# A hybrid encoder block on one core: the order of the steps in an attention slot, and of the first loads and squares

## The chip, the cores and the metric

The kernel runs on one core of one Trainium2 chip, in one launch. The metric is the device time of that launch in microseconds (us), lower is better. TensorE (PE in the profile) multiplies matrices from SBUF into PSUM; its weight loads have a row of their own (PEld). ScalarE (ACT) and VectorE (DVE) read and write both memories. SyncE (SP) issues all loads and stores. Each engine works through its own queue in order, and semaphores tie the queues together.

## The reference

One encoder block on x (1024 tokens by 1024 features, float32), one layer:

```
h = rms_norm(x);  proj = h @ w_in          # 13 projections in one product
y_gla = gated linear attention, forward and backward, 4 heads, chunked
y_swa = softmax attention in a window of +-128, 8 heads on 2 key/value heads
x = x + (sigmoid(gate_a) * y_gla + sigmoid(gate_b) * y_swa) @ w_out
x = x + swiglu(rms_norm(x))                # feed-forward of width 2816
```

The softmax attention works on blocks of 128 queries, each against its own block of keys and the two beside it, with normed and rotated q and k and a learned sink logit per head:

```
scores = q . k / sqrt(128), masked to the window
m = max(scores.max, sink);  p = exp(scores - m)
o = (p / (p.sum + exp(sink - m))) @ v
```

## The kernel before, in words

**Arithmetic.** Every float32 matrix product is done as three matmuls. An operand a is split into a high part (ScalarE copies it into a rounded type, `wh`, `xh`, `qh`, `ph`) and a low part (VectorE subtracts the high part from the original, `wl`, `xl`, `ql`, `pl`), and `mm3` (lines 74 to 77) adds high x high, high x low and low x high in PSUM. `wunit` (lines 62 to 69) loads one weight tile of 128 x 512 and splits it so.

**Engines' orders.** Nearly all is written inside `tc.manual_schedule(engines={PE})`: TensorE's order is the order of the program text. The other engines' instructions are ordered by a scheduler at build time, from readiness and their place in the text. Tiles of a pool with one tag share `bufs` buffers; a new tile waits until an old one's last reader is done. PSUM holds two tags of four banks each: `mm` for the dense products and `ch` for the small ones.

**First stage (lines 263 to 306).** x is held transposed, as 8 feature tiles k by 2 halves s of 512 tokens, 256 KB each. For each k and s, `x_tile` loads the half tile, ScalarE makes `xh` (line 266, with the norm's gain as a scale), VectorE makes `xl` (line 267), ScalarE squares x (line 271) and VectorE adds the square to `acc` (line 273). TensorE then does 6 matmuls for the half tile: the first two dense projections (q and k of head 0), three matmuls each. The weight tiles of these two are loaded ahead of k = 0 and of k = 4 (line 279). After the loop come the low-rank gate product (`lr_mm`, 24 matmuls on line 72 into `ch`, in two halves), and between the halves the norm's statistics: a matmul of ones with `acc` (line 120, `norm_stats`).

**Dense work as filler.** All further projections are generators in the list `dense`. `fill(n)` takes the next n dense matmuls from it. `slot(stages, n)` (lines 230 to 238) runs the given stages one after the other and after each of them puts its share of n dense matmuls, so that TensorE has work while the other engines prepare the next stage. The gated linear attention (lines 310 to 502) and the softmax attention are both run in this way. Weight tiles of the dense work are loaded and split two tiles ahead (`next_unit`, lines 158 to 161).

**Softmax attention (lines 505 to 683).** The units are 16 pairs (g, n): a group g of four heads and a block n of 128 queries. One pair passes through six slots:

- slot n: `k_prep` (keys and values of the block, only while g = 0): load, value split, norm and rotation
- slot n + 1: `a_prep`: load of the four heads' q, sum of squares (line 531), rotation into `a.qn` (lines 587 to 592); `k_turn` (g = 0): transposes of the key block (line 573) and their split
- slot n + 2: `a_turn`: four transposes of q (line 598) and their split into `a.qh`, `a.ql`
- slot n + 3: `a_scores`, four stages, one per head: three matmuls into a bank (line 614), then VectorE adds the band mask, writes p and takes the row maximum (line 615). After the fourth head: the maximum with the sink (lines 622 to 624), four exponentials on ScalarE (line 630), the sum and its reciprocal on VectorE (lines 632 and 634), and four scalings of p on ScalarE (line 636)
- slot n + 4: `a_probs`, three stages, one per key block: four transposes of p (line 647), split into `ph` (ScalarE, line 650) and `pl` (VectorE, line 651)
- slot n + 5: `a_out`: nine matmuls of p with the values, a copy by ScalarE (line 661) and four stores

A slot thus holds stages of up to six different pairs. Their order within the slot is the tuple `order` (line 677), by which each slot's list is sorted (line 680). A slot has 46 dense matmuls, 60 in the first two and 28 in the last four. With g = 0 there are 12 stages in a slot, with g = 1 ten. p (line 605) and the row maxima (line 606) have two buffers each.

The rest, the two output projections, the merge, and the feed-forward block (done with seven products in place of eight per pair of blocks), follows from line 686 on and is not touched.

Of the kernel before, what the change touches and what calls it, by code (L numbers as in the profile page):

```python
# [8 lines left out]
F32 = mybir.dt.float32  # L9
FR = mybir.dt.float32r  # L10
U32 = mybir.dt.uint32
AF = mybir.ActivationFunctionType
ALU = mybir.AluOpType

P = 128
T = 1024
KT = 8
HT = 512
# [11 lines left out]
def body(tc, i, out):  # L30
    nc = tc.nc
    with ExitStack() as root:
# [8 lines left out]
        def nm(s):  # L41
            uid[0] += 1
            return f"{s}_{uid[0]}"

        def mmtile(shape=(P, 512), dt=F32):
            return psm.tile(list(shape), dt, tag="mm", name=nm("mm"))

        def chtile(shape, dt=F32):
            return psc.tile(list(shape), dt, tag="ch", name=nm("ch"))
# [7 lines left out]
        def load_const(pool, name, src, shape, dt=F32):  # L57
            t = pool.tile(list(shape), dt, tag=name, name=name)
            nc.sync.dma_start(out=t, in_=src)
            return t  # L60

        def wunit(src, n=512):
            raw = wp.tile([P, n], F32, tag="wr", name=nm("wr"), bufs=4)
            nc.sync.dma_start(out=raw, in_=src)
            h = wp.tile([P, n], FR, tag="wh", name=nm("wh"), bufs=5)
            nc.scalar.activation(h, raw, AF.Copy)  # L66
            l = wp.tile([P, n], FR, tag="wl", name=nm("wl"), bufs=5)
            nc.vector.tensor_tensor(l, raw, h.bitcast(F32), op=ALU.subtract)  # L68
            return h, l

        def mm(o, a, b, start, stop):
            nc.tensor.matmul(o, a, b, start=start, stop=stop)  # L72

        def mm3(o, ah, al, bh, bl, start, stop):
            mm(o, ah, bh, start, False)
            mm(o, ah, bl, False, False)
            mm(o, al, bh, False, stop)
# [3 lines left out]
        g1 = load_const(cst, "g1", i["g1"], (P, KT))  # L81
# [26 lines left out]
        xh = [[xp.tile([P, HT], FR, tag=f"xh{k}{s}", name=f"xh{k}{s}") for s in range(2)] for k in range(KT)]  # L108
        xl = [[xp.tile([P, HT], FR, tag=f"xl{k}{s}", name=f"xl{k}{s}") for s in range(2)] for k in range(KT)]
# [5 lines left out]
        ip = ini.enter_context(tc.tile_pool(name="ip", bufs=1))  # L115
# [131 lines left out]
        def lr_mm(b, u):  # L247
            h, l = wunit(i["w_lr"][u], 384)
            for kk in range(4):
                k = u * 4 + kk  # L250
                c = slice(kk * 96, (kk + 1) * 96)
                for s in range(2):
                    mm3(b[s][:96], h[:, c], l[:, c], xh[k][s], xl[k][s], k == 0, k == KT - 1)

        def lr_out(b):
# [4 lines left out]
            nc.scalar.activation(lrS[0:96], lrf, AF.Copy)  # L260
            nc.vector.tensor_tensor(lrS[32:64], lrf[32:64], lrS[32:64].bitcast(F32), op=ALU.subtract)

        def x_tile(k, s):
            xr = ip.tile([P, HT], F32, tag="xr", name=nm("xr"), bufs=8)
            nc.sync.dma_start(out=xr, in_=i["xT"][k, s])
            nc.scalar.activation(xh[k][s], xr, AF.Copy, scale=g1[:, k:k + 1])  # L266
            nc.vector.scalar_tensor_tensor(xl[k][s], xr, g1[:, k:k + 1], xh[k][s].bitcast(F32),  # L267
                                           op0=ALU.mult, op1=ALU.subtract)
            a = acc[:, s * HT:(s + 1) * HT]
            sq = a if k == 0 else ip.tile([P, HT], F32, tag="sq", name=nm("sq"), bufs=3)  # L270
            nc.scalar.activation(sq, xr, AF.Square)
            if k:
                nc.vector.tensor_tensor(a, a, sq, op=ALU.add)

        with tc.manual_schedule(engines={mybir.EngineType.PE}):
            bq = [[mmtile(), mmtile()] for _ in range(2)]
            for k in range(KT):
                if k % 4 == 0:
                    us = [wunit(i["w_f"][m, k // 4]) for m in range(2)]
                c = slice((k % 4) * P, (k % 4 + 1) * P)  # L280
                for s in range(2):
                    x_tile(k, s)
                    for m in range(2):
                        mm3(bq[m][s], us[m][0][:, c], us[m][1][:, c], xh[k][s], xl[k][s], k == 0, k == KT - 1)
            ident = load_const(cst, "ident", i["c_ident"], (P, P))
            tri = load_const(gc, "tri", i["c_tri"], (P, P), U32)
            g2 = load_const(cst, "g2", i["g2"], (P, KT))
            og = load_const(cst, "og", i["og"], (P, 2))
            bl = [chtile((P, 512)), chtile((P, 512))]
            lr_mm(bl, 0)  # L290
            norm_stats(acc, ip)
            vt = chtile((P, KT, 2))
            for t in range(KT):
                mm(vt[:, t], acc[:, t * P:(t + 1) * P], ones[:, 0:2], True, True)
            lr_mm(bl, 1)
            proj_f_out("q0", bq[0])
            proj_f_out("k0", bq[1])
            rsqrt(rstdt, vt[:, :, 0], 1.0 / T, EPS, epst, ip, (P, KT), "rt")
            upr = ip.tile([98, 2, 512], F32, tag="upr", name="upr")
            nc.sync.dma_start(out=upr, in_=i["up"])  # L300
            nc.scalar.activation(upS, upr, AF.Copy)
            nc.vector.tensor_tensor(upS[64:98], upr[64:98], upS[64:98].bitcast(F32), op=ALU.subtract)
            nc.scalar.activation(upS[96:97], upr[96:97], AF.Copy)
            nc.vector.memset(lrS[96:98].bitcast(F32), 1.0)
            lr_out(bl)
# [201 lines left out]
        sw = swas.enter_context(tc.tile_pool(name="swt", bufs=2))  # L507
# [86 lines left out]
        def a_turn(g, n):  # L594
            a = att[g, n]
            qt = chtile((P, 4, P))
            for h in range(4):
                nc.tensor.transpose(qt[:, h], a.qn[:, h], ident)
            a.qh = sw.tile([P, 4, P], FR, tag="qh", name=nm("sqh"))
            a.ql = sw.tile([P, 4, P], FR, tag="ql", name=nm("sql"))  # L600
            nc.scalar.activation(a.qh, qt, AF.Copy)
            nc.vector.tensor_tensor(a.ql, qt, a.qh.bitcast(F32), op=ALU.subtract)
            a.b0, a.b1 = max(n - 1, 0), min(n + 1, KT - 1)
            a.w = (a.b1 - a.b0 + 1) * P
            a.p = sw.tile([P, 4, 384], F32, tag="p", name=nm("p"))
            a.mx = sw.tile([P, 4], F32, tag="mx", name=nm("mx"))

        def a_scores(g, n, h):
            a = att[g, n]
            w, p, mx = a.w, a.p, a.mx  # L610
            ks = slice(a.b0 * P, (a.b1 + 1) * P)
            mo = (a.b0 - (n - 1)) * P
            s = chtile((P, 384))
            mm3(s[:, :w], a.qh[:, h], a.ql[:, h], kTh[:, g, ks], kTl[:, g, ks], True, True)
            nc.vector.tensor_tensor_reduce(out=p[:, h, :w], in0=s[:, :w], in1=band[:, mo:mo + w],
                                           op0=ALU.add, op1=ALU.max, scale=1.0, scalar=-1e30,
                                           accum_out=mx[:, h:h + 1])
            if h < 3:
                return
            sk = sink[:, 4 * g:4 * g + 4]  # L620
            nm_ = sw.tile([P, 4], F32, tag="nm", name=nm("nm"))
            nc.vector.tensor_tensor(mx, mx, a.rs, op=ALU.mult)
            nc.vector.tensor_tensor(mx, mx, sk, op=ALU.max)
            nc.vector.tensor_scalar(nm_, mx, -1.0, None, op0=ALU.mult)  # L624
            es = sw.tile([P, 4], F32, tag="es", name=nm("es"))
            nc.vector.tensor_tensor(es, sk, mx, op=ALU.subtract)
            nc.scalar.activation(es, es, AF.Exp)
            dn = sw.tile([P, 4], F32, tag="dn", name=nm("dn"))
            for h in range(4):
                nc.scalar.activation(p[:, h, :w], p[:, h, :w], AF.Exp, bias=nm_[:, h:h + 1],  # L630
                                     scale=a.rs[:, h:h + 1], accum_out=dn[:, h:h + 1])
            nc.vector.tensor_tensor(dn, dn, es, op=ALU.add)
            rd = sw.tile([P, 4], F32, tag="rd", name=nm("rd"))
            nc.vector.reciprocal(rd, dn)
            for h in range(4):
                nc.scalar.activation(p[:, h, :w], p[:, h, :w], AF.Copy, scale=rd[:, h:h + 1])  # L636
# [30 lines left out]
        for n in range(2 * KT):  # L667
# [6 lines left out]
            if n < KT:  # L674
                todo[n + 1].append((k_turn, n))
                todo[n].append((k_prep, n))
        order = (a_out, a_probs, a_scores, a_turn, k_turn, k_prep, a_prep)
        with tc.manual_schedule(engines={mybir.EngineType.PE}):
            for t, v in enumerate(todo):
                v.sort(key=lambda e: order.index(e[0]))  # L680
# [514 lines left out]
```

## Time and profile before

| what | value |
|---|---|
| median of 3 runs | 1697.69 us (1697.48 to 1699.71) |
| the profiled execution | 1697.71 us |
| its span, first to last instruction | 1695.6 us |
| TensorE matmuls busy | 1675.2 us, 7880 instructions |
| weight loads busy | 1388.9 us |
| VectorE busy | 1179.8 us |
| ScalarE busy | 867.8 us |

The first stage runs up to about 50 us, the gated linear attention to about 440 us, the softmax attention to about 750 us, the output projections to about 1070 us, the feed-forward block to the end.

In the rows of a timeline the first number is the start in us from the span's start, the second the duration of the row in us, then the engine, the source line, the operation, what is written and what is read, the shapes and the number of merged instructions; in square brackets stands how long the engine had been idle and what let it go. In the groups by line, the numbers behind the bar are busy us, mean ns of one instruction, and idle us of the engine just before them with what ended it. A matmul's shown duration is longer than the distance to the next one's start, since matmuls overlap in the array; lost time on TensorE is read best from starts.

### The profile page before, as it was taken

The page shows a single profiled execution, that of the slowest core. Times are in us where ns is not written, and L with a number is a line of the kernel's source. Part 1 is how long each engine was busy: PE and PEld are TensorE (multiplying, and loading weights), DVE is VectorE, ACT ScalarE, POOL GpSimd, SP SyncE. Part 2 cuts the span into 40 slices and gives each one's busy share as a digit, 9 for nine tenths or more (in the row PEclk, how much of TensorE's full clock was granted, in tenths as well). Part 3 has the DMA queues.
Part 4 walks back from the last instruction along what each step waited for, and adds up shares of the span by engine and source line. Part 5 has one row for each costly group of instructions (what it writes and reads, how often), then busy time and mean ns, then how long its engine had stood idle before and what let it go on. Part 6 is the DMA issues. An engine that isn't in the chain of part 4 may idle for free.

```text
span 1695.6 us, 23682 instructions
## 1 busy us (share of the span) xinstructions
PE 1675.2 (99%) x7880; PEld 1388.9 (82%) x7880; DVE 1179.8 (70%) x2454; ACT 867.8 (51%) x1939; POOL 0.2 (0%) x4
## 2 busy tenths in 40 slices
PE   8999999999999999999999999999999999999999
PEld 6788888888788878878888888888888888788887
DVE  7767777764577656537574468978778887779655
ACT  6554767775557565545453456633333333354443
POOL 0000000000000000000000000000000000000000
PEclk9999999999999999999999999999999999999999
DMA  6533444443543232237765645344223543496433
GB/s 196 156 112 111 121 130 135 132 143 119 177 128 108 82 106 81 82 108 249 237 200 168 192 137 180 116 128 149 88 94 131 172 157 129 138 342 200 142 106 118
DMA packets 153738, 245.85 MB, mean 145 GB/s; under 512 B 17582, under 2 KB 43054, under 8 KB 153616
## 3 DMA queue, kind: packets, MB, share of 16 engines
q1 hardware_dynamic: 153616, 244.34, 45.4%
q8 instruction: 62, 1.02, 0.3%
q14 instruction: 60, 0.49, 0.1%
HBM read 177.17 MB, written 67.11 MB: 144 GB/s over the span
## 4 chain that ended last, share of the span: by engine, by line
PE 92%; DVE 3%; ACT 3%; DMA 1%; issue 1%; SPq 0%; ACTq 0%; DVEq 0%
PE mm L72 46%; PE ch L72 8%; PE mm L1012 6%; PE mm L865 6%; PE mm L866 6%; PE mm L867 6%; PE ch L1012 5%; PE ch L866 2%; PE ch L867 2%; PE ch L865 2%; PE ch L647 1%; ACT p L636 1%; ACT p L630 1%; PE ch L474 0%; PE ch L389 0%
## 5 line engine op out<-in xcount | busy, mean ns | idle before, releaser
L66 ACT ACTIVATE wh<-wr 128x512 fp32r<-128x512 f32 (+1 forms) x256 | 159.2, 626 | 173.6 <-PE mm L72 149.2
L68 DVE TENSOR_TENSOR wl<-wr,wh 128x512 fp32r<-128x512 f32 (+1 forms) x256 | 174.6, 685 | 92.6 <-ACT wh L66 88.0
L72 PE MATMUL mm<-xh,wh 128*128 128x512 f32 x512 | 204.1, 399 | 6.5 <-ACT xh L266 6.5
L72 PE MATMUL mm<-xl,wh 128*128 128x512 f32 x512 | 204.0, 398 | 0.0
L72 PE MATMUL mm<-xh,wl 128*128 128x512 f32 x512 | 169.7, 398 | 0.0
L72 PE MATMUL mm<-wh,xh 128*128 128x512 f32 x320 | 126.7, 396 | 1.9 <-DVE st L146 1.2
L72 PE MATMUL mm<-wl,xh 128*128 128x512 f32 x320 | 127.3, 398 | 0.0
L72 PE MATMUL mm<-wh,xl 128*128 128x512 f32 x320 | 126.3, 395 | 0.0
L72 PEld LDWEIGHTS mm<-xh,wh 128*128 128x128 f32 x512 | 97.0, 190 | 23.3 <-ACT xh L266 6.5
L839 ACT ACTIVATE wh<-ws 128x512 fp32r<-128x512 f32 x88 | 55.5, 632 | 115.9 <-PE mm L866 68.0
L72 PEld LDWEIGHTS mm<-xl,wh 128*128 128x128 f32 x512 | 97.2, 190 | 17.5 <-DVE xl L267 0.5
L72 PEld LDWEIGHTS mm<-xh,wl 128*128 128x128 f32 x512 | 95.3, 190 | 16.7
L839 ACT ACTIVATE wh<-a 128x512 fp32r<-128x512 f32 x66 | 41.7, 632 | 89.8 <-PE ch L1012 42.3
L839 ACT ACTIVATE wh<-wr 128x512 fp32r<-128x512 f32 x52 | 32.9, 632 | 91.6 <-issue 49.7
L840 DVE TENSOR_TENSOR wl<-a,wh 128x512 fp32r<-128x512 f32 x66 | 45.5, 690 | 41.6 <-ACT wh L839 41.4
L72 PEld LDWEIGHTS mm<-wh,xh 128*128 128x128 f32 x320 | 60.2, 188 | 13.9 <-DVE st L146 1.6
L630 ACT ACTIVATE p<-p,nm,rs 128x384 f32<-128x384 f32 (+1 forms) x64 | 42.9, 672 | 56.1 <-DVE nm L624 56.1
L1012 PE MATMUL mm<-hh,wh 128*128 128x512 f32 x176 | 68.6, 390 | 1.5 <-ACT hh L984 1.5
L1012 PE MATMUL mm<-hl,wh 128*128 128x512 f32 x176 | 68.7, 390 | 0.8 <-DVE hl L985 0.8
L840 DVE TENSOR_TENSOR wl<-ws,wh 128x512 fp32r<-128x512 f32 x88 | 60.1, 683 | 12.5 <-ACT wh L839 12.5
L72 PEld LDWEIGHTS mm<-wh,xl 128*128 128x128 f32 x320 | 60.2, 188 | 10.4
L1012 PE MATMUL mm<-hh,wl 128*128 128x512 f32 x176 | 68.6, 390 | 0.1
(508 smaller groups left out, 4420.6 us busy)
## 6 DMA issues: line engine op xcount, KB each, us to landing
wr<-in_w_fi_dram SPq DMA_DIRECT2D x102, 256.0 KB, 2.8
wr<-in_w_t_dram SPq DMA_DIRECT2D x80, 256.0 KB, 2.7
wr<-in_w_f_dram SPq DMA_DIRECT2D x64, 256.0 KB, 2.7
B<-c SPq DMA_DIRECT2D x44, 256.0 KB, 2.1
T<-tx SPq DMA_DIRECT2D x44, 256.0 KB, 2.3
a<-in_w_fo_dram SPq DMA_DIRECT2D x44, 256.0 KB, 5.3
hr<-T SPq DMA_DIRECT2D x44, 256.0 KB, 2.7
hr<-B SPq DMA_DIRECT2D x33, 256.0 KB, 4.6
```

What stands on the lines that cost most here:

```text
L66: nc.scalar.activation(h, raw, AF.Copy)
L68: nc.vector.tensor_tensor(l, raw, h.bitcast(F32), op=ALU.subtract)
L72: nc.tensor.matmul(o, a, b, start=start, stop=stop)
L630: nc.scalar.activation(p[:, h, :w], p[:, h, :w], AF.Exp, bias=nm_[:, h:h + 1], scale=a.rs[:, h:h + 1], accum_out=dn[:, h:h + 1])
L636: nc.scalar.activation(p[:, h, :w], p[:, h, :w], AF.Copy, scale=rd[:, h:h + 1])
L647: nc.tensor.transpose(pt[:, h], a.p[:, h, (kb - a.b0) * P:(kb - a.b0 + 1) * P], ident)
L839: nc.scalar.activation(h, src, AF.Copy)
L840: nc.vector.tensor_tensor(l, src, h.bitcast(F32), op=ALU.subtract)
L865: nc.tensor.matmul(o, h[:, c], x[kk][0], start=start and kk == 0, stop=False, skip_group_check=True)
L866: nc.tensor.matmul(o, h[:, c], x[kk][1], start=False, stop=False, skip_group_check=True)
L867: nc.tensor.matmul(o, l[:, c], x[kk][0], start=False, stop=kk == nk - 1, skip_group_check=True)
L1012: nc.tensor.matmul(ys[m], a[:, c], b, start=f0, stop=f1, skip_group_check=True)
```

## The change

Two separate edits. In the attention slot, the order of the steps: `k_prep` and `a_prep` go first, then the scores, the turns of q and k, and `a_out` and `a_probs` last; p and the maxima are allocated at the first scores instead of in `a_turn`. In the first stage, `x_tile` is cut into a load, a split and a square. The first half tile of x is loaded ahead of the first two weight tiles; the loads of tile k + 1 are issued ahead of the splits of tile k; each half tile has a buffer of its own (16, where 8 were shared); all squares and their sums come behind the loop, so behind all splits and in the text ahead of the low-rank product.

```diff
+        xr = {}
+
+        def x_load(k, s):
+            xr[k, s] = ip.tile([P, HT], F32, tag=f"xr{k}{s}", name=f"xr{k}{s}")
+            nc.sync.dma_start(out=xr[k, s], in_=i["xT"][k, s])
+
         def x_tile(k, s):
-            xr = ip.tile([P, HT], F32, tag="xr", name=nm("xr"), bufs=8)
-            nc.sync.dma_start(out=xr, in_=i["xT"][k, s])
-            nc.scalar.activation(xh[k][s], xr, AF.Copy, scale=g1[:, k:k + 1])
...
+        def x_square(k, s):
             a = acc[:, s * HT:(s + 1) * HT]
             sq = a if k == 0 else ip.tile([P, HT], F32, tag="sq", name=nm("sq"), bufs=3)
-            nc.scalar.activation(sq, xr, AF.Square)
+            nc.scalar.activation(sq, xr[k, s], AF.Square)
             if k:
                 nc.vector.tensor_tensor(a, a, sq, op=ALU.add)
...
+            x_load(0, 0)
+            us = [wunit(i["w_f"][m, 0]) for m in range(2)]
+            x_load(0, 1)
             for k in range(KT):
-                if k % 4 == 0:
-                    us = [wunit(i["w_f"][m, k // 4]) for m in range(2)]
+                if k < KT - 1:
+                    for s in range(2):
+                        x_load(k + 1, s)
+                if k == 4:
+                    us = [wunit(i["w_f"][m, 1]) for m in range(2)]
...
+            for k in range(KT):
+                for s in range(2):
+                    x_square(k, s)
...
-            a.p = sw.tile([P, 4, 384], F32, tag="p", name=nm("p"))
-            a.mx = sw.tile([P, 4], F32, tag="mx", name=nm("mx"))
 
         def a_scores(g, n, h):
             a = att[g, n]
+            if h == 0:
+                a.p = sw.tile([P, 4, 384], F32, tag="p", name=nm("p"))
+                a.mx = sw.tile([P, 4], F32, tag="mx", name=nm("mx"))
...
-        order = (a_out, a_probs, a_scores, a_turn, k_turn, k_prep, a_prep)
+        order = (k_prep, a_prep, a_scores, a_turn, k_turn, a_out, a_probs)
```

More of the change, by code (lines that the diff above doesn't have):

```diff
@@ L261, in lr_out @@
             nc.vector.tensor_tensor(lrS[32:64], lrf[32:64], lrS[32:64].bitcast(F32), op=ALU.subtract)
+        xr = {}
+        def x_load(k, s):
+            xr[k, s] = ip.tile([P, HT], F32, tag=f"xr{k}{s}", name=f"xr{k}{s}")
+            nc.sync.dma_start(out=xr[k, s], in_=i["xT"][k, s])
         def x_tile(k, s):
-            xr = ip.tile([P, HT], F32, tag="xr", name=nm("xr"), bufs=8)
-            nc.sync.dma_start(out=xr, in_=i["xT"][k, s])
-            nc.scalar.activation(xh[k][s], xr, AF.Copy, scale=g1[:, k:k + 1])
-            nc.vector.scalar_tensor_tensor(xl[k][s], xr, g1[:, k:k + 1], xh[k][s].bitcast(F32),
+            nc.scalar.activation(xh[k][s], xr[k, s], AF.Copy, scale=g1[:, k:k + 1])
+            nc.vector.scalar_tensor_tensor(xl[k][s], xr[k, s], g1[:, k:k + 1], xh[k][s].bitcast(F32),
                                            op0=ALU.mult, op1=ALU.subtract)
+        def x_square(k, s):
             a = acc[:, s * HT:(s + 1) * HT]
             sq = a if k == 0 else ip.tile([P, HT], F32, tag="sq", name=nm("sq"), bufs=3)
-            nc.scalar.activation(sq, xr, AF.Square)
+            nc.scalar.activation(sq, xr[k, s], AF.Square)
             if k:
```

## The prediction

> **What bounds the kernel now.** I read the page's first table, then the groups of instructions by line, then the timeline of one slot of the attention stage and of the first 37 us.
>
> ```profile
> span 1695.6 us, 23682 instructions
> ...
> PE 1675.2 (99%) x7880; PEld 1388.9 (82%) x7880; DVE 1179.8 (70%) x2454; ACT 867.8 (51%) x1939; POOL 0.2 (0%) x4
> ```
>
> TensorE carries the span: 1675.2 of 1695.6 us. An edit that leaves its matmuls alone, as this one does, can only win TensorE's waits. In the attention stage nearly all of them sit in front of one line, 647, the transposes of the probabilities (rows of the groups by line):
>
> ```profile
> L647 PE MATMUL ch<-ident,p 128*128 128x128 f32 x176 | 31.4, 281 | 2.8 <-ACT p L636 1.9
> L647 PEld LDWEIGHTS ch<-ident,p 128*128 128x128 f32 x176 | 22.5, 140 | 14.1 <-ACT p L636 8.4
> ```
>
> The two rows tell different sizes. TensorE's own idle time is 2.8 us; the weight loads (here p is the weight) stood 8.4 us waiting for line 636, ScalarE's scaling of p. The timeline settles which is lost (start, duration, engine; bracketed is idle time):
>
> ```profile
> 663.60 1.62 ACT L636 ACTIVATE p<-p,rd 128x384 f32<-128x384 f32 x3
> 663.93 0.66 PE L647 MATMUL ch<-ident,p 128*128 128x128 f32 x2
> 664.77 0.33 PE L647 MATMUL ch<-ident,p 128*128 128x128 f32 x1 [0.17 <-ACT p L636]
> ...
> 665.36 0.48 PE L72 MATMUL mm<-xh,wl 128*128 128x512 f32 x1
> ...
> 666.62 0.60 PE L647 MATMUL ch<-ident,p 128*128 128x128 f32 x4
> 666.97 0.71 PE L72 MATMUL mm<-xh,wl 128*128 128x512 f32 x2
> ```
>
> Four transposes that wait for nothing take 666.97 - 666.62 = 0.35 us to the next matmul, and show as 0.60 us busy. The four before them took 665.36 - 663.93 = 1.43 us, each let go by one scaling on ScalarE (1.62 / 3 = 0.54 us): 1.08 us lost, of which the idle column shows some 0.35 (0.17, and about as much at the fourth). Over the stage there are 176 / 4 = 44 groups of four, which unhindered would show 44 x 0.60 = 26.4 us busy; they show 31.4 + 2.8 idle, so 7.8 us is lost by that count and 8.4 by the weight loads' waits. I take 8.1.
>
> The Trainium skill, Perfetto Trace Analysis, section Identifying the Most-Contended Engine, says that matmul busy time is no good measure of what is left, because matmuls are pipelined, and that the weight loads' row is to be read. The trace agrees: 2.8 us by the one, 8.4 by the other, 7.8 by counting. By the idle row alone the attention part of my sum would be 2.8.
>
> **The change in the attention stage.** Work, instruction counts and the number of dense projection matmuls per slot stay the same; only the order within a slot changes. Why p is late now, from the same slot, for the second group of heads:
>
> ```profile
> 674.38 0.34 PE L72 MATMUL ch<-kTh,sqh 128*128 128x384 f32 x1
> ...
> 674.91 0.39 PE L72 MATMUL mm<-xl,wh 128*128 128x512 f32 x1
> ...
> 675.82 0.60 PE L598 MATMUL ch<-ident,qn 128*128 128x128 f32 x4
> ...
> 676.31 0.71 ACT L630 ACTIVATE p<-p,nm,rs 128x384 f32<-128x384 f32 x1 [4.68 <-DVE nm L624]
> ...
> 678.57 0.39 PE L72 MATMUL ch<-ph,vSh 128*128 128x512 f32 x1
> ...
> 679.19 0.58 ACT L601 ACTIVATE sqh<-ch 128x512 fp32r<-128x512 f32 x1
> ...
> 680.19 2.12 ACT L636 ACTIVATE p<-p,rd 128x384 f32<-128x384 f32 x4
> ...
> 681.60 0.58 PE L647 MATMUL ch<-ident,p 128*128 128x128 f32 x3
> ```
>
> The last scores leave TensorE at 674.91 (call it T). The exponentials start at T + 1.4 and the last scaling of p ends at 682.31, T + 7.4. TensorE wants the first p at 681.60, T + 6.7: between them lie only the turn of q, a_out and some fill. In the new order turn, k_turn, a_out and probs follow the scores, but these probs are of the block before. The p of T is asked for one slot later, after the next slot's scores, turn and a_out: a slot is 681.60 - 663.93 = 17.7 us with its waits, so at about T + 6 + 16.6 = T + 22.6, against T + 7.4. The wait goes whole, with 15 us to spare: -8.1 us.
>
> What is late next? p has two buffers. A block's p is written from its scores on and read by the probs one slot later; the block after next writes into it in the slot after that, behind the last transposes by the fill of one or two stages (about 1 us each: 46 dense matmuls over 10 stages at 0.23 us, the spacing in the first stage's rows below) and its own score matmuls (674.91 - 674.38 = 0.53). So p is free some 2 us early. That is why its allocation moves into a_scores; the moved line issues nothing. a_out now meets ph and pl of a whole slot before, a_turn meets a qn of a whole slot before. Both gain cover. k_prep and a_prep move to the head of a slot, with their loads on SP's queue; their readers, k_turn and a_turn, stand a slot later, as before.
>
> The narrow resource is the four PSUM banks of tag ch. Behind T they are taken by scores, turn, a_out, probs 0, then probs 1 (the scores' bank), probs 2 (the turn's), the next scores 0 (a_out's). Summing 1.06 us of fill per stage, 0.35 a group of four and 9 x 0.23 = 2.1 for a_out, the next scores come at T + 11. a_out's bank must by then have been copied by ScalarE: in the row order above it follows the scalings, 682.31 + 0.56 = T + 8.0. Cover 3 us; if it is gone, each us more costs one per slot.
>
> ```profile
> L650 ACT ACTIVATE ph<-ch 128x512 fp32r<-128x512 f32 x44 | 26.1, 594 | 8.3 <-PE ch L647 8.0
> L66 ACT ACTIVATE wh<-wr 128x512 fp32r<-128x512 f32 x32 | 20.0, 626 | 41.7 <-PE mm L72 41.6
> L661 ACT COPY sob<-ch 128x512 f32<-128x512 f32 x15 | 8.5, 564 | 0.0
> L531 ACT ACTIVATE sq<-qr 128x128 f32<-128x128 f32 x44 | 13.1, 302 | 0.8 <-DMA qr<-sq 0.5 <-DVE sql L602 0.2 <-DVE qn L592 0.2
> L531 ACT ACTIVATION_READ_ACCUMULATOR sq<-qr 128x1 f32 x44 | 8.4, 191 | 0.0
> ```
>
> ScalarE has room: the weight splits of this stage (line 66) waited 41.7 us in all for TensorE to free their buffers, so they run well ahead. The four stores of a_out move on SP's queue from a slot's head to its middle; a weight load queued behind them may start some us later, into that same lead. I cost both at nothing; without that lead it would be up to 0.6 us a slot.
>
> **The change in the first stage.**
>
> ```profile
> 1.17 0.89 SPq L64 DMA_DIRECT2D wr<-in_w_f_dram  x2
> ...
> 3.90 1.39 ACT L66 ACTIVATE wh<-wr 128x512 fp32r<-128x512 f32 x2 [1.90 <-DMA wr<-in_w_f_dram]
> ...
> 5.68 0.72 ACT L266 ACTIVATE xh<-xr,g 128x512 fp32r<-128x512 f32 x1 [0.39 <-DMA xr<-in_xT_dram]
> ...
> 6.46 0.79 PE L72 MATMUL mm<-xh,wh 128*128 128x512 f32 x1 [6.46 <-ACT xh L266]
> ...
> 7.33 0.72 ACT L266 ACTIVATE xh<-xr,g 128x512 fp32r<-128x512 f32 x1 [0.41 <-DMA xr<-in_xT_dram]
> ...
> 9.54 0.63 PE L72 MATMUL mm<-xh,wh 128*128 128x512 f32 x1
> ...
> 12.10 0.63 PE L72 MATMUL mm<-xh,wh 128*128 128x512 f32 x1
> 12.53 0.45 PE L72 MATMUL mm<-xl,wh 128*128 128x512 f32 x1
> ...
> 13.29 0.39 PE L72 MATMUL mm<-xl,wh 128*128 128x512 f32 x1
> 13.52 0.39 PE L72 MATMUL mm<-xh,wl 128*128 128x512 f32 x1
> ```
>
> The queue of loads was weight, weight, x, x; it becomes x, weight, weight, x. All are of one size, so places 1 to 3 land when they do now: 3.9, 4.66 (the second split of the 1.39 us pair), 5.68. The x split runs 3.90 to 4.62, the first weight's 4.66 to 5.29, and TensorE starts 0.06 later (as 6.46 follows 6.40) at 5.35 instead of 6.46: 1.1 us earlier. The second weight's split ends by 6.31; its matmuls are fourth in line, at about 7.1. The fourth load keeps its place: split by 8.05 as now, wanted at 5.35 + (9.54 - 6.46) = 8.43. So no new wait.
>
> What 1.1 us is worth depends on the clock: starts are 0.43 us apart until 12.53 and 0.23 after. If full speed comes that much earlier too, 1.1 us; if it comes at 12.5 all the same, the 1.1 us hold matmuls at half rate, 1.1 x 0.23 / 0.43 = 0.6. I take 0.8.
>
> The Trainium skill, TensorE: Matmul & The Clock Gate, section Part 1: The HAM clock gate (the "warmup" mystery), says that the clock is let go after one busy window of about 3.4 us that runs freely, whatever the kernel does. The trace agrees as far as it goes: 6.1 us passed from the first matmul to 12.53, within one to two windows. By the page the start would be worth an estimated 0.6 to 2.2 us, by the phase of each run.
>
> The squares now stand behind all 16 splits of x (the first fence gives min/median/max of a line in ns, the second is the timeline).
>
> ```profile
> L266 ACT ACTIVATE xh<-xr,g x16: 707/709/722, 5.7 to 24.3; 128x512 fp32r<-128x512 f32 x16
> ...
> L271 ACT ACTIVATE sq<-xr x14: 613/617/619, 9.1 to 24.9; 128x512 f32<-128x512 f32 x14
> ```
>
> ```profile
> 28.13 0.56 DVE L68 TENSOR_TENSOR wl<-wr,wh 128x384 fp32r<-128x384 f32 x1
> ...
> 31.91 0.39 PE L72 MATMUL ch<-xh,wl 128*96 128x512 f32 x1
> ...
> 36.99 1.02 PE L72 MATMUL ch<-acc,ones 128*128 128x512 f32 x2
> ```
>
> ScalarE's splits of x (16 x 0.71) and of four weights (4 x 0.63) take 13.9 us from 3.9, with about 1 us of waiting for x's second half: 18.8. Sixteen squares at 0.62 end at 28.7, the last sum on VectorE 0.7 later, 29.4. The sums are read at 36.99 (now 36.2): 6.8 us of cover. Queued behind them on VectorE is the split of the low-rank weights, at 28.13 now, then by 30.0, wanted at 31.91 - 0.8 = 31.1: cover 1.1 us. Cost nothing; if that cover is gone, up to 1 us, once. Every half tile of x has a buffer of its own, so SP's queue no longer stops for them: a gain for the loads behind, worth nothing while TensorE has its weights.
>
> **Sum.** -8.1 - 0.8 = -8.9. The profiled execution took 1697.71 us, its span of 1695.6 and 2.1 around it, and is the median of the runs (1697.69): 1688.8 us.
>
> **The rivals.**
> *Half of it is given back.* Once TensorE no longer pauses about 0.5 us a slot, something that this pause covered is late next: a bank whose copy on ScalarE stands behind the eight softmax instructions. For it: 679.19 shows the turn's copy running only after the exponentials, though its transposes ended at 676.42. Against: the cover of 3 us. Half of 8.1 kept: 1697.7 - 4.0 - 0.8 = 1692.9.
> *No change.* ScalarE and VectorE are put in another order by the scheduler that arranges them, and waits of the present size turn up elsewhere, or the pauses of TensorE that the idle row shows (2.8) were all there was to win and the start loses what it should gain: 1695 to 1697.
> *Slower.* In each slot the softmax, the two weight splits (1.25), the four squares with their reads (4 x 0.49 = 2.0) and the three copies of probs (1.8) run ahead of a_out's copy: 5.0 us later, 2 beyond the cover. Sixteen slots lose 32, less 8.9: 1720.8. It decides from 3.6 us of delay, where 16 x 0.6 eats the gain. Against it: ScalarE idles 4.68 us ahead of the exponentials at 676.31, so such work has gone by then. The Trainium skill, TensorE: Matmul & The Clock Gate, section Architectural detail: the array is 16× 32×32, calls ScalarE's and VectorE's queues strictly first in, first out; the copy at 679.19 agrees. By that rule nothing lets a_out's copy pass what stands ahead of it.
> *The start doesn't do what it says.* The weight splits keep their place ahead of x's on ScalarE, though x lands first: 6.31 + 0.72 and TensorE starts at 7.1, 0.6 later than now, some 0.5 us lost in place of 0.8 won: 1690.1. It lies within the forecast's own range.
>
> **How the numbers follow.** Forecast 0.70 (0.15 of it with the start failing), own range 1687.0 to 1691.5; half given back 0.13; no change 0.10; slower 0.07. The low end is 1686.8: 8.4 for the waits, 2.2 for the start, 0.3 of scatter. The high end takes in the half and reaches into no change: 1695.0. What a measurement can tell from no change is 0.2%, 3.4 us, so faster means under 1694.3: the forecast and most of the half, 0.80; no change and the rest of the half 0.13; slower 0.07.
>
> **What would show it.** Right: the weight loads of line 647 wait under 1 us in all for line 636, its matmuls show about 26.4 us busy; the first matmul starts at about 5.4 us; no new group in the stage has more than 1 us of idle time on PE or behind a DVE or ACT release. Wrong: PE or PEld rows of lines 72, 598 or 647 waiting for ob, ph or p, or a wait for line 273 ahead of the sums.

## The result, and the profile after

| | time | runs |
|---|---|---|
| before | 1697.88 us (1697.48 to 1699.71) | 4 |
| changed | 1688.74 us (1688.22 to 1689.21) | 4 |
| ratio | 0.9944, 95% interval 0.9927 to 0.9961 | |

The change gains 9.1 us; the prediction said 8.9. The profiled execution of the changed kernel took 1689.21 us, with a span of 1687.4. The first lines of its page:

```profile
span 1687.4 us, 23673 instructions
...
PE 1670.9 (99%) x7880; PEld 1390.1 (82%) x7880; DVE 1181.0 (70%) x2454; ACT 869.3 (52%) x1939; POOL 0.2 (0%) x4
```

TensorE's 7880 matmuls are the same in number, and the work of the other engines has hardly changed. The transposes of p, line 647 before, stand on line 664 now; the scaling of p is line 653, the exponential 647, the copy of a_out 678. The two rows that the attention term was read from, in the groups by line of the changed kernel:

```profile
L664 PE MATMUL ch<-ident,p 128*128 128x128 f32 x176 | 26.4, 272 | 0.0
...
L664 PEld LDWEIGHTS ch<-ident,p 128*128 128x128 f32 x176 | 21.9, 140 | 6.0
```

The matmuls show 26.4 us and no idle time, where they showed 31.4 and 2.8; the weight loads no longer wait for ScalarE. For the 6.0 us left the view names no releaser; the 14.1 before held 5.7 of that kind beside the 8.4. The timeline of one slot shows why. The last scores of a block end at about 646.0 us, T:

```profile
645.88 0.34 PE L72 MATMUL ch<-kTh,sql 128*128 128x384 f32 x1
...
648.41 0.70 ACT L647 ACTIVATE p<-p,nm,rs 128x384 f32<-128x384 f32 x1
...
651.10 0.60 PE L664 MATMUL ch<-ident,p 128*128 128x128 f32 x4
651.19 0.57 ACT L678 COPY sob<-ch 128x512 f32<-128x512 f32 x1
...
651.79 2.14 ACT L653 ACTIVATE p<-p,rd 128x384 f32<-128x384 f32 x4
...
667.68 0.60 PE L664 MATMUL ch<-ident,p 128*128 128x128 f32 x4
```

The scalings end at 653.93, T + 7.9 (forecast T + 7.4). The transposes at 651.10 are those of the block before; this p's own stand at 667.68, T + 21.6 (forecast T + 22.6). About 14 us lie between. In a stretch of the stage away from its ends, the table of windows has PE without any idle time. Its columns are the stretch, its length, then busy us and instructions of PE, PEld, DVE, ACT and POOL, the clock, the DMA share and GB/s; first the kernel before, then the changed one:

```profile
484.00:753.00 269.00, 266.19 (x1317) 219.97 (x1317) 163.32 (x493) 157.11 (x451) 0.00 (x0) 1.00 0.28 89
```

```profile
484.00:753.00 269.00, 269.00 (x1354) 226.62 (x1353) 166.46 (x504) 160.29 (x465) 0.00 (x0) 1.00 0.31 96
```

**Where the time came from.** TensorE's program order outside the attention slots is unchanged, so the same matmul, by its number in that order, can be looked up in both traces. Number 2300 stands just ahead of the attention stage, number 4000 behind it. Before:

```profile
452.05 0.39 PE L72 MATMUL mm<-xh,wh 128*128 128x512 f32 x1
...
807.49 0.39 PE L72 MATMUL mm<-oah,wh 128*128 128x512 f32 x1
```

and changed:

```profile
451.45 0.39 PE L72 MATMUL mm<-xh,wh 128*128 128x512 f32 x1
...
798.37 0.39 PE L72 MATMUL mm<-oah,wh 128*128 128x512 f32 x1
```

The changed kernel is 0.60 ahead when the attention stage begins and 9.12 ahead when it has ended: 8.5 us come from the stage, 0.6 from all before it. One more us is lost behind: in the feed-forward block both kernels wait some 2 us for the split of the hidden values at the same matmul, and after it the changed kernel's matmuls start 0.43 apart for 3.41 us. That leaves 8.2 of the span. By medians the gain is 9.1; single executions differ by a us or so, which is why the parts were measured by themselves.

The start in the changed kernel's timeline (forecast: first matmul at 5.35):

```profile
4.05 0.72 ACT L270 ACTIVATE xh<-xr,g 128x512 fp32r<-128x512 f32 x1 [2.04 <-DMA xr<-in_xT_dram]
4.68 0.62 ACT L277 ACTIVATE acc<-xr 128x512 f32<-128x512 f32 x1
...
5.20 1.16 ACT L66 ACTIVATE wh<-wr 128x512 fp32r<-128x512 f32 x2
...
5.87 0.80 PE L72 MATMUL mm<-xh,wh 128*128 128x512 f32 x1 [5.87 <-ACT wh L66]
...
9.02 0.51 PE L72 MATMUL mm<-xl,wh 128*128 128x512 f32 x1
...
9.37 0.39 PE L72 MATMUL mm<-xh,wl 128*128 128x512 f32 x1
```

TensorE starts at 5.87, not 5.35: x and the first weight landed later than assumed, and the first square slipped in between the split of x and that of the weight. The matmul during which full speed comes is that at 9.02, 3.5 us sooner than the one at 12.53 before. Near 40 us most of that lead goes again:

```profile
40.00 0.63 PE L72 MATMUL ch<-xh,wh 128*96 128x512 f32 x1
...
42.99 0.58 PE L72 MATMUL ch<-xl,wh 128*96 128x512 f32 x1
43.40 0.40 PE L72 MATMUL ch<-xh,wl 128*96 128x512 f32 x1
```

Eight matmuls start 0.43 apart, where before none did. By matmul numbers the lead is 2.08 us at the end of the first stage's loop and 0.47 at 56 us. The profiler also records the granted clock of TensorE, the share of full speed that it was let run at. It is the column "clock" of the table of windows, and it is half for just this stretch of the changed kernel, behind one at full speed:

```profile
36.55:39.96 3.41, 2.76 (x20) 2.35 (x20) 1.63 (x4) 1.22 (x4) 0.00 (x0) 1.00 0.28 77
39.96:43.37 3.41, 3.41 (x9) 2.22 (x8) 3.31 (x8) 1.32 (x2) 0.00 (x0) 0.50 0.17 63
```

The stretch behind the wait in the feed-forward block, 1473.56 to 1476.97 us, is one of the same length and the same half clock.

### The profile page after: what moved, and what is told of

The parts are those of the page before. It is cut to its first block, busy times and chain, and to the rows that moved or that the text cites. A ratio compares the mean times of both kernels' runs of the same rounds, so it can differ in the third digit from the quotient of the medians.

```text
span 1687.4 us, 23673 instructions
## 1 busy us (share of the span) xinstructions
PE 1670.9 (99%) x7880; PEld 1390.1 (82%) x7880; DVE 1181.0 (70%) x2454; ACT 869.3 (52%) x1939; POOL 0.2 (0%) x4
## 4 chain that ended last, share of the span: by engine, by line
PE 97%; DVE 2%; ACT 1%; DMA 0%; issue 0%; SPq 0%; ACTq 0%; DVEq 0%
PE mm L72 48%; PE ch L72 9%; PE mm L1029 7%; PE mm L884 6%; PE mm L882 6%; PE mm L883 6%; PE ch L1029 5%; PE ch L884 2%; PE ch L882 2%; PE ch L883 2%; PE ch L664 1%; PE ch L490 0%; PE ch L614 0%; PE ch L405 0%; DVE cs L364 0%
```

## The experiments

The question was whether the 9 us are the attention edit (theory: p was asked for too soon after its scores, so the distance in slots is what counts) or partly the start, and whether anything of it is given back. Ratios are to the kernel before, timed on the same chip beside each run, with 95% intervals.

| run | us (range, runs) | ratio |
|---|---|---|
| attention edit alone | 1691.06 (1690.11 to 1691.57, 4) | 0.9957 [0.9943, 0.9970] |
| the same, again | 1690.88 (1689.86 to 1691.32, 5) | 0.9956 [0.9944, 0.9969] |
| start edit alone | 1697.88 (1696.24 to 1698.21, 10) | 0.9994 [0.9985, 1.0004] |
| the same, again | 1695.98 (1695.36 to 1697.99, 11) | 0.9988 [0.9979, 0.9997] |
| changed kernel again | 1688.40 (1688.02 to 1690.10, 5) | 0.9944 [0.9931, 0.9958] |
| changed, squares from the last tile on | 1688.49 (1688.34 to 1688.61, 5) | 0.9942 [0.9930, 0.9955] |
| changed, squares back behind each split | 1690.34 (1688.75 to 1690.74, 4) | 0.9949 [0.9932, 0.9966] |
| before, x's first half tile loaded first | 1697.60 (1696.01 to 1698.59, 11) | 0.9993 [0.9985, 1.0002] |
| before, old order, p used a slot later | 1691.12 (1689.81 to 1691.91, 4) | 0.9957 [0.9943, 0.9970] |
| changed, 4 more copies per block on ScalarE | 1690.67 (1689.12 to 1691.25, 3) | 0.9951 [0.9935, 0.9966] |
| changed, 8 more copies per block | 1699.87 (1698.41 to 1701.55, 8) | 1.0009 [0.9999, 1.0020] |
| before, 4 more copies per block | 1723.71 (1723.21 to 1724.20, 2) | 1.0149 [1.0128, 1.0169] |

**The attention edit alone**, on the kernel before (the allocation of p and the maxima moves as in the change):

```diff
-        order = (a_out, a_probs, a_scores, a_turn, k_turn, k_prep, a_prep)
+        order = (k_prep, a_prep, a_scores, a_turn, k_turn, a_out, a_probs)
```

> The attention edit alone (order of the steps in a slot, p allocated at the first scores), first stage as before. Theory: the loss was TensorE waiting for the scaled p at the transposes, so this part alone wins about 8.5 us, some 1689.3 us; the weight loads of the transposes wait under 1 us for the scalings and their matmuls show about 26.4 us busy; the first matmul starts at 6.5 us. Rival: only the 2.8 us that TensorE's idle column shows were to win, some 1695 us. Rival: most of the gain came from the first stage, then this stays above 1695 us as well.

It took 1691.06 us, 7.4 under the 1698.45 of its neighbours. The groups by line of this run:

```profile
L648 PE MATMUL ch<-ident,p 128*128 128x128 f32 x176 | 26.3, 272 | 0.0
L648 PEld LDWEIGHTS ch<-ident,p 128*128 128x128 f32 x176 | 21.9, 141 | 6.0
```

They match the rows of the changed kernel. By matmul numbers 2300 to 4000, the stage is 8.5 us shorter than before; the missing 1.1 of the total go in the start (first matmul at 7.10 us, 0.64 later than in the profiled execution of before) and behind the wait in the feed-forward block.

**The start edit alone** is the rest of the change (the cut of `x_tile` and the order of loads and squares), on the kernel before.

> The first stage's edit alone (loads and squares), attention order as before. Theory: the first matmul starts at 5.9 us instead of 6.5, and the time is 0.5 us less, 1697.3 us, give or take 1 us by when the clock comes up and whether it dips; the transposes of p keep their 8 us of waits. Rival: the first stage carries the gain, then some 1690 us.

1697.88 us, 0.6 under its neighbours, within what can be told from nothing. The transposes of p wait as before, here 8.9 us of their weight loads:

```profile
L663 PE MATMUL ch<-ident,p 128*128 128x128 f32 x176 | 31.6, 281 | 3.1 <-ACT p L652 2.4
L663 PEld LDWEIGHTS ch<-ident,p 128*128 128x128 f32 x176 | 22.6, 140 | 14.6 <-ACT p L652 8.9
```

So the attention's waits belong to the order alone. But the two parts come to 8.0 by medians against 9.1 together, and the changed kernel is 2.3 under the attention edit alone, so the size of the start term stayed open; later runs come back to it.

**Order or distance?** This run keeps the old order and moves `a_probs` and `a_out` one slot on instead (p and the maxima allocated at the first scores, as in the change):

```diff
-        todo = [[] for _ in range(2 * KT + 6)]
+        todo = [[] for _ in range(2 * KT + 7)]
...
-            todo[n + 5].append((a_out, g, t))
-            todo[n + 4] += [(a_probs, g, t, kb) for kb in range(3)]
+            todo[n + 6].append((a_out, g, t))
+            todo[n + 5] += [(a_probs, g, t, kb) for kb in range(3)]
```

> The kernel before with its old order of steps, but probs and a_out each one slot later and p allocated at the first scores. It gives p the cover of a whole slot without the new order. Theory: distance between scores and transposes is all that counts, so the waits at the transposes go as they do with the new order, about 8 us less, some 1689.5 us. Rival: the new order wins by something else as well (preparation first, banks in another sequence), then this stays 2 us or more above the order-only run.

1691.12 us against 1691.06 for the new order alone, the stage 8.3 us shorter than before, and the transposes show 26.3 us busy and no idle. What was gained is distance between the scores and the transposes: got in this other way, it gains the same.

**How much cover there is now.** ScalarE was given more to do between scaling and use: four copies of p onto itself per block, then eight, which change no value. The expectations put them at 2.2 and 4.3 us a slot, from the length of the scalings. In the traces a copy starts 0.41 us behind the one before, so four hold ScalarE 1.65 us and eight 3.3, and less in the blocks at the ends, where p is narrower.

```diff
                 nc.scalar.activation(p[:, h, :w], p[:, h, :w], AF.Copy, scale=rd[:, h:h + 1])
+            for h in range(4):
+                nc.scalar.activation(p[:, h % 4, :w], p[:, h % 4, :w], AF.Copy)
```

> The changed kernel with four more copies of p onto itself on ScalarE behind the scalings of each block (2.2 us per slot, p unchanged). Theory: p has some 15 us of cover now and the PSUM banks 3 us, so this costs under 1 us in all: 1688.5 to 1690. Rival: ScalarE's order is the next bound and each slot pays for part of it: 10 us or more.

Four copies: 1690.67 us, 1.9 over the changed kernel, 1.9 in the stage by the trace too. p was not waited for; the waits that appeared are 0.3 us for a_out's copy, 0.5 for `ph` and 0.2 for `pl`. So copies of 1.65 us, well inside the 3 us of cover that the prediction estimated for the banks, were not quite free.

> The changed kernel with eight more such copies (4.3 us per slot). By the cover that the prediction gave the banks (3 us, now over-drawn by 1.3) each of 16 slots pays 1.3 us: some 1709 us, with TensorE waiting for copies of banks (ob or ph), not for p. Rival: the cover is larger than that, since a_out's copy goes ahead of the scalings in the changed kernel's trace (it ended at 651.76, the scalings began at 651.79): then under 3 us, 1689 to 1692.

Eight copies (`range(8)` in the same loop): 1699.87 us, 11.1 over the changed kernel, so all the gain is gone. In the groups by line of this run, again nothing waits for p:

```profile
L666 PE MATMUL ch<-ident,p 128*128 128x128 f32 x176 | 26.5, 273 | 3.5 <-ACT sob L680 3.5
...
L72 PE MATMUL ch<-ph,vSh 128*128 128x512 f32 x44 | 18.0, 408 | 3.0 <-ACT ph L669 3.0
```

TensorE waits for ScalarE's copies out of PSUM, as the prediction's list of what would show it wrong had it (ob, ph or p); but not once in every slot. The timeline has four places, near 558, 578, 711 and 740 us, of which the largest two run like this:

```profile
558.30 0.40 PE L72 MATMUL mm<-xh,wh 128*128 128x512 f32 x1
560.69 0.66 PE L666 MATMUL ch<-ident,p 128*128 128x128 f32 x4 [1.99 <-ACT sob L680]
...
562.51 0.63 PE L72 MATMUL mm<-xh,wh 128*128 128x512 f32 x1
562.94 0.63 PE L72 MATMUL mm<-xl,wh 128*128 128x512 f32 x1
...
740.36 0.40 PE L72 MATMUL ch<-ph,vSl 128*128 128x512 f32 x1
743.73 0.80 PE L72 MATMUL ch<-ph,vSh 128*128 128x512 f32 x1 [2.97 <-ACT ph L669]
744.46 0.80 PE L72 MATMUL ch<-pl,vSh 128*128 128x512 f32 x1
```

Counted by starts beyond a free matmul's distance, the four waits cost 2.2, 1.7, 0.5 and 3.1 us, 7.5 together; most of the other 5 of the 12.5 us that the stage lost are matmuls 0.43 apart behind the first and the last of them. The rule "1.3 us of shortage in each of 16 slots" is wrong, and so is the rival that expected nearly no loss.

The changed kernel's own trace tells how much cover these places had. The matmul that waits at 560.69 above, looked up there by its number, starts at 558.22:

```profile
554.15 2.14 ACT L653 ACTIVATE p<-p,rd 128x384 f32<-128x384 f32 x4
...
556.46 0.57 ACT L678 COPY sob<-ch 128x512 f32<-128x512 f32 x1
...
558.22 0.60 PE L664 MATMUL ch<-ident,p 128*128 128x128 f32 x4
```

The copy of a_out that it waits for ends at 557.03, so the cover was 1.2 us. At the waits near 578 and 711 us it was 1.7 and 2.8. In these three slots the copy follows the scalings on ScalarE, so eight copies of 3.3 us put it 2.1, 1.6 and 0.5 us beyond the cover, and the waits cost 2.2, 1.7 and 0.5. The cover is not one number for all slots: only the roomiest of these three came near the prediction's 3 us. The cover of the fourth wait, for a `ph` in the last slot, stays open.

**The same load on the old order**: the four copies, on the kernel before.

> The kernel before with four more copies of p per block (2.2 us per slot). Theory: there p is what TensorE waits for, so a slot that waited pays all of it (11 of 16 did) and the others what goes beyond their small cover: 11 x 2.2 = 24 and some 5 more, about 1727 us, shown as waits at the transposes. Rival: TensorE's wait was something that merely ended with p, and the cost is under 10 us.

1723.71 us, 25.6 over its neighbours, where the changed kernel paid 1.9 for the same copies:

```profile
L649 PE MATMUL ch<-ident,p 128*128 128x128 f32 x176 | 37.7, 298 | 16.9 <-ACT p L638 14.1
L649 PEld LDWEIGHTS ch<-ident,p 128*128 128x128 f32 x176 | 23.7, 144 | 35.8 <-ACT p L638 31.3 <-issue 0.6
```

The weight loads wait 31.3 us for line 638, 22.9 more than the 8.4 before; the idle column of the matmuls grows by only 14.1, and the rest shows as longer busy time, 37.7 for 31.4. The copies hold ScalarE some 26 us over the 16 blocks (26.2 us busy). In the old order most of that delay in ScalarE's softmax is TensorE's; in the new one little is. Up to 3 of the 25.6 us are not waits: this trace has two stretches of 3.41 us at half clock, near 700 and 772 us.

**The squares.** Two runs went into what their place is worth. First the squares from the last half tile to the first, so that none is ready when the first split of x ends (the sum is the same but for the order of its terms):

```diff
-            sq = a if k == 0 else ip.tile([P, HT], F32, tag="sq", name=nm("sq"), bufs=3)
+            sq = a if k == KT - 1 else ip.tile([P, HT], F32, tag="sq", name=nm("sq"), bufs=3)
...
-            if k:
+            if k < KT - 1:
...
-            for k in range(KT):
+            for k in reversed(range(KT)):
                 for s in range(2):
                     x_square(k, s)
```

> The changed kernel, with the squares written from the last tile of x to the first, so that the first half tile's square cannot slip in between x's split and the first weight's split on ScalarE. Theory: that square (0.62 us) is why TensorE started at 5.87 and not near 5.35; without it ScalarE splits the weight as it lands (4.86 in the profiled run), TensorE starts at about 5.55, 0.3 us earlier, time 0 to 0.5 us under the changed kernel. Rival: the squares all come later now, and the sums end late enough that TensorE waits for acc or for the low-rank weights' split: slower by up to 2 us.

1688.49 us, the changed kernel's time. In its trace the first weight's split begins 0.07 us after its load has landed, where the changed kernel's begins 0.34 after, so the square that slips in does delay the start; but this execution's x landed 0.4 later, and nothing of it is left in the total.

Then each square back behind its own split, the rest as changed:

```diff
                     x_tile(k, s)
+                    x_square(k, s)
                     for m in range(2):
                         mm3(bq[m][s], us[m][0][:, c], us[m][1][:, c], xh[k][s], xl[k][s], k == 0, k == KT - 1)
-            for k in range(KT):
-                for s in range(2):
-                    x_square(k, s)
```

> The changed kernel with each square back behind its own split of x, the loads ahead as changed. Theory: the earlier first matmul comes from the load order alone; TensorE starts at about 5.8 us here too and the time is the changed kernel's within 0.5 us. Rival: the squares' place is what let the splits run ahead: then TensorE waits for x's splits in the first stage and the time is 1 us or more longer.

1690.34 us, 1.6 to 1.9 over the changed kernel's two medians, with ranges that overlap. In its trace I find 0.33 us of a later first matmul, 0.43 of a later rise of the clock and a wait of 0.6 us near 74 us for a split whose load is late. The first two vary between runs of one kernel; the wait stands in none of the other traces. The extra time may be the place of the squares; it is not shown.

**Again, side by side.** The changed kernel and the attention edit alone on one chip:

> The changed kernel itself, beside the order-only kernel on the same chip: what the first stage's edit is worth on top of the other. The three traces with the old load order start TensorE at 6.46, 7.10 and 7.74 us, the three with the new at 5.87, 5.77 and 5.74. Theory: the edit is worth the mean of that, 1.3 us, at full or half clock, so 0.7 to 1.3 us: 1688.7 us here against 1689.4 to 1691 in the order-only kernel. Rival: it is worth nothing that outlasts the clock's phase, then the two medians agree within 0.5 us.

> The order-only kernel once more, on the same chip as the changed kernel. Theory: 0.7 to 1.3 us (at most 2.3, as in the runs before) over the changed kernel; TensorE starts when the third load in the queue has landed and been split, later than 6.4 us. Rival: within 0.5 us of it.

1688.40 and 1690.88: 2.5 us apart, 2.3 the first time. The start edit alone, and its first load alone, on one chip:

> The first stage's edit alone, once more. On top of the new order the edit was worth 2.3 and 2.5 us in two pairs of medians, alone it was worth 0.6 us in one. Theory: one and the same worth, since the stages do not touch: 1.5 to 2.5 us under the kernel before, 1696 to 1696.8 us against its 1698.3. Rival: alone it is worth under 1 us, because the attention stage of the old order takes part of it back (its waits for p were 8.7 us in the start-only trace against 8.2 to 8.4).

> The kernel before with one thing changed: x's first half tile is loaded ahead of the first two weight tiles. Buffers, squares and all other loads as before. Theory: the start hangs on the third load's landing; with x first TensorE starts at 5.8 to 6.6 us, as in the seven traces with the new loads, and this alone is worth what the whole edit of the first stage is, within 0.5 us. Rival: the squares' place and the free buffers give a good part of it (the squares-in-place run was 1.6 to 1.9 us over the changed kernel): then it stands 1 us or more above the start-only run.

The last one's edit loads only x's first half tile ahead of the weights, on the kernel before:

```diff
+        def x_first():
+            xr = ip.tile([P, HT], F32, tag="xr", name=nm("xr"), bufs=8)
+            nc.sync.dma_start(out=xr, in_=i["xT"][0, 0])
+            return xr
+
         def x_tile(k, s):
-            xr = ip.tile([P, HT], F32, tag="xr", name=nm("xr"), bufs=8)
-            nc.sync.dma_start(out=xr, in_=i["xT"][k, s])
+            xr = x0 if k + s == 0 else ip.tile([P, HT], F32, tag="xr", name=nm("xr"), bufs=8)
+            if k + s:
+                nc.sync.dma_start(out=xr, in_=i["xT"][k, s])
...
+            x0 = x_first()
```

The start edit took 1695.98, 2.4 under its neighbours' 1698.37; the first load alone 1697.60, 0.8 under. Both bring the first matmul to 5.6 to 5.8 us. So by medians the earlier first matmul alone was worth less than the whole edit, but the times of each kernel lie in two groups some 1.5 to 2 us apart, and a median says mostly which group has more runs. What sets the groups apart is on record: the granted clock of every run, averaged over its span. A stretch of 3.41 us at half clock takes 0.001 off it (0.5 x 3.41 / 1690), and in every trace the average fits the number of such stretches counted there. Sorted by it, the runs of that chip are (mean us, and runs in brackets):

| granted clock over the span | before | start edit | first load alone |
|---|---|---|---|
| 1.000, no stretch at half clock | 1697.78 (12) | 1695.87 (8) | 1696.13 (4) |
| 0.999, one | none | 1697.29 (1) | 1697.15 (2) |
| 0.998, two | 1699.49 (9) | 1697.80 (2) | 1698.18 (5) |

At the same granted clock the start edit stands 1.7 to 1.9 us under the kernel before, and the first load alone 1.3 to 1.7. So most of what the edit is worth comes with its first load. The difference between the two, at most 0.4, is small against the spread within a group (the 12 runs of the kernel before at 1.000 lie within 2.8 us), and no run shows that the squares' place and the free buffers add anything. Sorted in the same way, the first measurement of the start edit gives 1.5 us less at 1.000, 0.1 at 0.999 and 1.1 at 0.998, from two to seven runs each.

The stretches at half clock are not tied to the change: the attention edit alone and the slot-later run, both with the old start, show one near 40 us too, and the changed kernel's repeat, the same program as the changed kernel, shows none there. Its first matmul comes at 5.88 us against 5.87 and its full speed later, which puts it 1.27 us behind at the end of the loop; yet from 56 us on it is 0.34 ahead, because it lacks the eight slow matmuls at 40.

What the repeats do show is where the prediction's reading of the start came from. With the old order of loads, the first split of x began at 5.68 us in the kernel before; in the repeat of the attention edit, which leaves the start alone:

```profile
6.73 0.72 ACT L266 ACTIVATE xh<-xr,g 128x512 fp32r<-128x512 f32 x1 [1.40 <-DMA xr<-in_xT_dram]
```

and in the kernel before with four copies, whose start is the same too:

```profile
7.59 0.72 ACT L266 ACTIVATE xh<-xr,g 128x512 fp32r<-128x512 f32 x1 [2.16 <-DMA xr<-in_xT_dram]
```

The load is third in the queue. Over five traces with the old order TensorE's first matmul came at 6.46, 7.10, 7.51, 7.74 and 8.36 us, mean 7.43; over the nine with x first at 5.63 to 6.60, mean 5.9. The execution that the prediction was read from was the earliest of its five.

## Why the prediction was right, point by point

- **The waits of the transposes, -8.1.** Right in mechanism and in size. The stage gained 8.5 us between the same two matmuls in both traces, the transposes show the 26.4 us busy that was counted, and the same edit alone gives 7.4 to 7.5 us of time. Reading the idle column alone would have said 2.8. What counted was the distance of starts and the weight loads' wait.
- **The wait goes whole, with some 15 us to spare.** Right: 13.7 us in the slot shown, and neither four nor eight copies on ScalarE made TensorE wait for p. That it is the distance and not the new order as such is shown by the run that keeps the old order one slot later.
- **Half given back; no change; slower by a_out's copy.** None happened in the changed kernel: in the stretch shown PE is never idle. In the slot shown a_out's copy (651.19) runs ahead of the scalings, but in ten of the fourteen slots that have both it follows them, as the prediction reckoned (556.46, behind scalings that end at 556.29), and still comes in time. The mechanism of the slower rival is real, as eight copies show: the banks are the next bound.
- **"Each us more costs one per slot."** Wrong. With eight copies, 3.3 us more on ScalarE, four places waited, not 16, for 7.5 us, and behind two of them matmuls started 0.43 apart. With 1.65 us more, inside the estimated cover, 1.9 us were lost. The step took one cover of 3 us for all slots; in three of the places that waited it was 1.2, 1.7 and 2.8 us.
- **Squares and the low-rank split.** Right: in the changed kernel the sums end at 27.6 us (forecast 29.4) and the low-rank weights' split starts at 27.49 (forecast by 30.0); nothing waits for either.
- **The start, -0.8.** The mis-sized term. In pairs it is worth 2.3 and 2.5 us (changed kernel against the attention edit), and alone 0.6 and 2.4; alone and at the same granted clock, 1.7 to 1.9 in the repeat and 0.1 to 1.5 the first time. The working held three assumptions that one trace could not show: that places 1 to 3 of the queue land when they did in that execution (typically the earlier first matmul is 1.5 us, 7.43 to 5.9, not 1.1); that nothing comes between the two splits on ScalarE (a square did, for about 0.3); and that the clock's rise is all the clock does here (it rose 3.5 us sooner and fell again near 40 us).

  The Trainium skill's page TensorE: Matmul & The Clock Gate, section Part 1: The HAM clock gate (the "warmup" mystery), from which the prediction took an estimate of 0.6 to 2.2 us by the phase of each run, is nearer to these pairs than the 0.8 taken from one trace's rows. The traces agree with its window of about 3.4 us that runs freely: by the record of the granted clock, full speed came 3.4 us after the first matmul in the changed kernel, 6.2 in the kernel before, and 3.6 to 6.4 in the other twelve traces.
- **The total, 8.9 forecast and 9.1 measured**, agrees better than its terms, and that is in part luck: by medians the order is worth 7.4 to 7.5 and the start 2.3 to 2.5, not 8.1 and 0.8. In the trace 8.5 come from the stage, and up to 1 us of that goes in the clock behind the wait in the feed-forward block.

No version tried is clearly faster than the changed kernel; the one with the squares reversed equals it.

## What to carry to other kernels

A wait of a transposed or weight operand hides in the matmuls' busy time: count it by the distance of starts against an unhindered group, or by the weight loads' row, before costing the edit that takes it away. In a cyclic schedule, put the consumer behind the next round's producer, a whole slot away, and move the buffer's allocation with it; then look for the next bound in what the same engine copies out of PSUM. When a term hangs on when a load lands, one trace is one draw: read it from several executions. And before two medians a us or two apart are compared, sort the runs by their granted clock.

## What the runs showed of the hardware

- TensorE fell to matmuls 0.43 us apart, from 0.23, after short pauses in the middle of the kernel: behind a wait of 1.99 us, and for longer behind one of 2.97, in the run with eight copies; and in the changed kernel behind a wait of 0.65 us and 16 matmuls of two columns near 37 us. A wait of 1.55 us (near 579 us in the run with eight copies) was not followed by it. Each time the record shows the granted clock at 0.50 for 3.41 us, and for 6.83 behind the wait of 2.97:

```profile
562.12:565.53 3.41, 3.41 (x10) 2.91 (x9) 2.07 (x6) 2.16 (x11) 0.00 (x0) 0.50 0.40 101
743.03:749.85 6.82, 6.12 (x14) 4.43 (x15) 1.98 (x3) 2.24 (x5) 0.00 (x0) 0.50 0.10 29
```

So a pause can cost more than its length: 3.41 us with matmuls 0.43 apart in place of 0.23 lose an estimated 1.6 us, and in that run 7.5 us of waiting took about 5 more. Which pause is followed by it changes between executions, and the traces show by what. In all fourteen, every stretch at half clock begins a whole number of lengths of 3.413 us after the clock first rose (in the changed kernel 9.24 us, and 9 lengths later 39.96). The pause near 37 us, 2.45 us from the start of its wait to the end of its 16 small matmuls, is the same in every trace. In the seven with a stretch at half clock behind it, 2.1 us or more of it lie within one such length; in the other seven a boundary cuts it, and at most 1.8 us do. The Trainium skill, TensorE: Matmul & The Clock Gate, section HAM oscillation — how this bites in real kernels, gives as the rule that TensorE should have no idle gaps over about 3.4 us; here gaps of 1.99 and 2.97 us were enough.
- The landing of the third 256 KB load, issued some 2 us into the kernel, varied by 1.9 us between executions, read by the split that waits for it (5.68 to 7.59).
